# Split weights at staggered addresses in a two-layer encoder: 64 bytes for the MLPs' upward products, 192 for the value projection

## The chip, the cores and the metric

The kernel runs on one core of one Trainium2 chip. The metric is the time of one execution on the device in microseconds, as the median of several runs. TensorE multiplies, VectorE, ScalarE and GpSimd do the rest, and the DMA queues of SyncE and GpSimd bring the weights.

## What is computed

An encoder of two layers over 512 tokens of width 1024, in float32. The first layer mixes by stick-breaking attention (16 heads of 64), the second by a gated linear recurrence. Behind each mixer stands an MLP of width 4096 with a squared ReLU. Cut to what matters:

```python
def reference(x, ...):
    for layer in range(2):
        h = rms_norm(x, norm_mix[layer])
        if layer % 2 == 0:
            y = stick_breaking_attention(h, sb_w_qkv[0], sb_w_o[0])   # qkv = h @ w_qkv, ..., o @ w_o
        else:
            y = rglru_block(h, rg_w_in[0], ..., rg_w_o[0])
        x = x + y
        h = rms_norm(x, norm_mlp[layer])
        x = x + squared_relu_mlp(h, mlp_w1[layer], mlp_w2[layer])
    return rms_norm(x, norm_final)

def squared_relu_mlp(h, w1, w2):
    u = jax.nn.relu(h @ w1)
    return (u * u) @ w2
```

## The kernel before

**Split products.** A float32 product is made of three in the type float32r. Each operand `a` is split into a high part `ah` (ScalarE's cast, line 213 or, in the MLPs, line 1026 by way of the recording helper at line 755) and a low part `al` (VectorE's subtraction). TensorE then adds `wh*ah`, `wl*ah` and `wh*al` into one PSUM bank. Each of the three loads its stationary operand, 128 columns, and streams its moving operand, 512 or 256 columns.

**Widths and roles.** The dense products of the attention, the recurrence and the output projections (lines 220 to 222) load weights and stream 512 tokens. The MLPs' downward products (line 1061) load activations and stream 512 columns of weights. Two kinds stream 256 columns:

- The MLPs' upward products (`up`, line 966) load weights, `wh` or `wl`, and stream 256 tokens of `xgh`, `xgl` or a sum of blocks of them (`s41`, `low`, parts of `bh` and `bl`). The MLP multiplies 2x2 blocks by seven products in place of eight (`P1` to `P7`), hence the halves of 256. One named product is 24 matmuls.
- The value projection (`v_steps`, lines 476 to 478) loads 128 tokens of `xgh` or `xgl` and streams 256 columns of weights.

**Where the weights lie.** `wh` and `wl` are tiles of 8 x 128 float32r a partition, 4096 bytes, in the pool `wpool` with four buffers for each name. They are made by `slab_parts` (the first weights), `slab` (most of the attention and the first quarter of each MLP), `weights_high` (the recurrence, where a second pool `wmore` helps) and `operand` (the MLPs' seven products, downward and upward). In this layout every operand of the split products starts on a multiple of 512 bytes in its partition.

**The squares' sums.** For the norms, `Squares.acc` and the first layer's `sums` gather sums of squares in a tile `ssq` of 2048 bytes, which has a buffer of its own in the pool `work`. The same pool has two buffers each of `sq` and `r`.

**Order.** TensorE's order is the order in which the code issues. An MLP runs in quarters: 14 named products downward, 14 upward, and so on; `prepare` makes split weights four steps ahead. The order on VectorE and ScalarE inside the MLPs is fixed by the helper `Ordered` (line 755).

Of the kernel before, what the change touches and what calls it, by code (L numbers as in the profile page):

```python
# [11 lines left out]
F32 = mybir.dt.float32  # L12
F32R = mybir.dt.float32r
# [4 lines left out]
P = 128  # L18
S = 512
D = 1024  # L20
C = D // P
# [14 lines left out]
CUT = 2  # L36
# [25 lines left out]
def hybrid_encoder(  # L62
# [28 lines left out]
    wpool = ctx.enter_context(tc.tile_pool(name="wpool", bufs=4))  # L91
    work = ctx.enter_context(tc.tile_pool(name="work", bufs=2))
# [5 lines left out]
    def bank(tag=None):  # L98
        if tag is None:
            tag = TAGS[turn[0] % len(TAGS)]  # L100
            turn[0] += 1
        return psum.tile([P, S], F32, tag=tag, name=f"ps_{tag}")

    def f(ap):
        return ap.bitcast(F32)
# [36 lines left out]
    class Squares:  # L142


        def __init__(self):
            self.acc = work.tile([P, S], F32, tag="ssq", name="ssq", bufs=1)
            self.begun = False

        def chunk(self, c, xc, last=None, pool=None, e=V):
            if not self.begun:  # L150
                self.begun = True
                A.activation(self.acc, xc, AF.Square)
            else:
                sq = (pool or work).tile([P, S], F32, tag="sq", name="sq")
                A.activation(sq, xc, AF.Square)
                with tc.issue_after(last.ins) if last else nullcontext():
                    self.last = e.tensor_tensor(self.acc, self.acc, sq, ALU.add)
# [18 lines left out]
            return rr  # L176


    def slab_parts(src, cuts):

        raw = wpool.tile([P, C, P], F32, tag="raw", name="raw", bufs=3)
        wh = wpool.tile([P, C, P], F32R, tag="wh", name="wh")
        wl = wpool.tile([P, C, P], F32R, tag="wl", name="wl")

        def fetch(i, queue=nc.sync):
            k = slice(*cuts[i : i + 2])
            queue.dma_start(out=raw[:, k, :], in_=src[:, k, :])

        def part(i, high=A.copy):
            k = slice(*cuts[i : i + 2])  # L190
            if high:
                high(wh[:, k, :], raw[:, k, :])
            if high == V.tensor_copy:
                return
            V.tensor_tensor(wl[:, k, :], raw[:, k, :], f(wh[:, k, :]), ALU.subtract)

        return wh, wl, fetch, part
# [2 lines left out]
    slabs, loads = count(), count()  # L200
    behind = [None]

    def slab(src, cut=1, ks=range(C)):
        raws = rawpools[next(loads) % len(rawpools)]
        raw = raws.tile([P, C, P], F32, tag="raw", name="raw", bufs=3 if raws is wpool else 1)
        k = slice(ks.start, ks.stop)
        nc.sync.dma_start(out=raw[:, k, :], in_=src[:, k, :])
        pool = wpools[next(slabs) % len(wpools)]
        wh = pool.tile([P, C, P], F32R, tag="wh", name="wh")
        wl = pool.tile([P, C, P], F32R, tag="wl", name="wl")  # L210
        for i in range(cut):
            k = slice(ks.start + i * len(ks) // cut, ks.start + (i + 1) * len(ks) // cut)
            A.copy(wh[:, k, :], raw[:, k, :])  # L213
            with tc.issue_after(behind[0]) if behind[0] else nullcontext():
                V.tensor_tensor(wl[:, k, :], raw[:, k, :], f(wh[:, k, :]), ALU.subtract)  # L215
        return wh, wl
# [7 lines left out]
    def dense(src, ah, al, tag=None, halves=None, ks=range(C), ps=None):  # L224

        wh, wl = halves or slab(src, ks=ks)
        ps = bank(tag) if ps is None else ps
        for k in ks:
            three(ps, ah[:, k, :], al[:, k, :], wh[:, k, :], wl[:, k, :], k == ks[0], k == ks[-1])
        return ps  # L230
# [49 lines left out]
    NB = S // P  # L280
    PAIRS = H // 2
    half = [slice(0, HD), slice(HD, P)]
    so, early = {}, {}
# [7 lines left out]
    with ExitStack() as actx:  # L291
        hp = actx.enter_context(tc.tile_pool(name="hp", bufs=2))
# [11 lines left out]
        for i in range(2):  # L304
            both = []
            for nm in ("h", "l"):
                t = sp.tile([P, 2 * P], F32R, tag=f"last{nm}{i}", name=f"last{nm}{i}")
# [10 lines left out]
        q, kh, kl, v, w = {}, {}, {}, {}, {}  # L318
# [65 lines left out]

        xcs = [home_tile(tag, n, "x0") for tag, n in HOMES]
        parts = [slab_parts(w_qk[i, 0], (0, 2, 4, 6, 8)) for i in range(2)]
        parts += [slab_parts(w, (0, 4, 8)) for w in (w_qk[0, 1], w_qk[1, 1], w_v[0, 0], w_v[0, 1])]
        first = [bank("acc") for _ in range(2)]

        sums = work.tile([P, S], F32, tag="ssq", name="ssq", bufs=1)  # L390
        odd = hp.tile([P, S], F32, tag="ks", name="odd", bufs=1)
        sqs = [sums, odd, *(sc[:, :S] for sc in scans)]
        sqs += [work.tile([P, S], F32, tag=tag, name="sq") for tag in ("sq", "sq", "r")]
# [65 lines left out]
        def v_steps(m, tags=("acc",) * NB):  # L459

            if m:
                ws = [slab(w_v[m, i], CUT) for i in range(2)]
            else:
                ws = [u[:2] for u in parts[4:]]
                for u, name in zip(parts[4:], ("root", "copy")):

                    with tc.issue_after(norm[name].ins):
                        for i in range(2):
                            u[3](i)
            ws = [[t.rearrange("p (k two) f -> p k (two f)", two=2) for t in u] for u in ws]  # L470
            for t in range(NB):
                ts = slice(t * P, (t + 1) * P)
                ps = bank(tags[t])[:, : 2 * P]
                for k in range(C):
                    wh, wl = (u[:, k % 4, :] for u in ws[k // 4])
                    PE.matmul(ps, xgh[:, k, ts], wh, start=k == 0, stop=False)
                    PE.matmul(ps, xgh[:, k, ts], wl, start=False, stop=False)
                    PE.matmul(ps, xgl[:, k, ts], wh, start=False, stop=k == C - 1)
                    if k == C - 1:
                        vt = hp.tile([P, 4, P], F32R, tag=f"v{t}", name=f"v{t}")  # L480
                        pv = ps.rearrange("p (h d) -> p h d", h=4)
                        rc = norm["rc"][:, t : t + 1]
                        A.activation(vt[:, :, :HD], pv, AF.Identity, scale=rc)
                        V.scalar_tensor_tensor(
                            vt[:, :, HD:], pv, rc, f(vt[:, :, :HD]), ALU.mult, ALU.subtract
                        )
                        v[m, t] = vt
                    if k % 2:
                        yield
# [199 lines left out]
        steps = chain(*(g for g, _ in fill))  # L689
# [75 lines left out]
    class Mlp:  # L765
# [252 lines left out]
                self.FROM_UP,  # L1018
            )

        def operand(self, raw):
            pool = wpools[next(slabs) % len(wpools)]
            wh = pool.tile([P, C, P], F32R, tag="wh", name="wh")
            wl = pool.tile([P, C, P], F32R, tag="wl", name="wl")
            wh, wl = (t.rearrange("p (j k) f -> p j (k f)", j=2) for t in (wh, wl))
            self.A.copy(wh, raw)
            self.V.tensor_tensor(wl, raw, f(wh), ALU.subtract)
            return wh, wl
# [69 lines left out]
        def run(self, first, between, end):  # L1098
# [5 lines left out]
            steps = []  # L1104
# [5 lines left out]
            units, ws, sums, us = {("down", 0): first}, {}, {}, {}  # L1110
# [5 lines left out]
            def unit(i):  # L1116
                kind, q4, g, _ = steps[i]
                return units[kind, q4][g]

            done, made = set(), {}  # L1120
# [15 lines left out]
            def make(i):  # L1136
                if i >= len(steps):
                    return
                name = steps[i][3]
                ws[i] = made[i] = self.operand(self.source(unit(i), name))  # L1140

                for before, x in (("P5", "P7"), ("P6", "P4")):
                    if name == before:
                        self.added(unit(i), x)
# [107 lines left out]

            waiting, later = [], []
            make(0)
            add(1)
            make(1)
# [122 lines left out]
    with ExitStack() as rctx:  # L1379
# [36 lines left out]
        r = None  # L1416
# [3 lines left out]
        ws = {"c2": third}  # L1420
        raws, fetched, made = {}, count(), count(3)
# [6 lines left out]

        def weights_high(key):
            pool = wmore if next(made) % 6 > 3 else wpool  # L1430
            wh = pool.tile([P, C, P], F32R, tag="wh", name="wh")
            wl = pool.tile([P, C, P], F32R, tag="wl", name="wl")
            ws[key] = wh, wl
            OA.copy(wh, raws[key])

# [58 lines left out]
        def high(c):  # L1494

            i = C - 4 + c % 4
            gin[c] = bh[:, i, :], bl[:, i, :]
            OA.copy(gin[c][0], xc[c])
# [78 lines left out]
        for k in range(C):  # L1577
            for c in range(4):
                ps, wh, wl = begun[c]
# [6 lines left out]
    with ExitStack() as mctx:  # L1586
        lp = mctx.enter_context(tc.tile_pool(name="last", bufs=1))
# [26 lines left out]

        A.activation(lp.tile([P, 1], F32, tag="rt", name="early"), eps_t, AF.Sqrt)

        ss = lp.tile([P, 104], F32, tag="ss", name="ss")[:, : 3 * NB]
        ss = ss.rearrange("p (t i) -> p t i", t=NB)
        bias = lp.tile([P, NB], F32, tag="bias", name="bias")

# [155 lines left out]
```

## Time and profile before

| | |
|---|---|
| median of 3 runs | 1042.69 us (1041.5 to 1043.37) |
| profiled execution | 1044.21 us, span 1042.4 us |
| granted TensorE clock, mean | 0.999 |
| upward products, line 966 | 2016 matmuls, 243.4 us |
| downward products, line 1061 | 1356 matmuls, 307.5 us |
| value products, lines 476 to 478 | 3 x 128 matmuls |
| VectorE, ScalarE busy | 82%, 67% |

The upward stages lie from 331 to 371, 409 to 450 and 488 to 528 us in the first MLP, and from 799 to 841, 879 to 919 and 957 to 998 us in the second. Between and beside them lie the downward stages, before 292 us the attention, and from 567 to 759 us the recurrence. A matmul's length in the profile is modelled, from its start to the end of its last column, and the next one starts before it ends; the pace is read from the distance of starts.

### The profile page before, as it was taken

How to read it: one execution, taken by the hardware profiler on the slowest of the kernel's cores; microseconds unless marked ns; L12 is line 12 of the kernel's file. 1: busy time of each engine (PE TensorE's matmuls, PEld its weight loads, DVE VectorE, ACT ScalarE, POOL GpSimd, SP SyncE). 2: the span in 40 equal slices, each digit the busy share in tenths (PEclk: the TensorE clock that was granted, in tenths of full speed). 3: DMA queues.
4: the chain of work that ended last, by engine and by line, in shares of the span. 5: the costliest groups of instructions: out<-in, count | busy, mean ns of one | idle time of the engine just before them, and what ended most of it. 6: DMA issues, size and time to landing. Idle time of an engine off the chain costs nothing.

```text
span 1042.4 us, 15858 instructions
## 1 busy us (share of the span) xinstructions
PE 1032.3 (99%) x5862; PEld 906.2 (87%) x5862; DVE 859.0 (82%) x1148; ACT 701.6 (67%) x1083; POOL 172.5 (17%) x239
## 2 busy tenths in 40 slices
PE   9999999999999999999999999999999999999997
PEld 7888888888888988988988888888888988988986
DVE  7888787848788898898899888984789798898897
ACT  6777676836776773773765799964755773863866
POOL 0444444410010010010011121200000010010013
PEclk9999999999999999999999999999999999999999
DMA  7744454528546667667682575353446677677553
GB/s 242 209 117 142 111 152 104 160 93 294 139 78 188 184 136 205 162 137 200 152 222 78 153 189 144 102 222 90 93 80 173 173 143 199 163 144 196 150 128 109
DMA packets 53260, 160.46 MB, mean 154 GB/s; under 512 B 6720, under 2 KB 8256, under 8 KB 53184
## 3 DMA queue, kind: packets, MB, share of 16 engines
q1 hardware_dynamic: 42096, 120.35, 35.5%
q0 software_dynamic: 10656, 38.80, 22.8%
q8 instruction: 46, 0.75, 0.3%
q10 hardware_dynamic: 432, 0.31, 0.1%
q14 instruction: 30, 0.25, 0.1%
HBM read 137.41 MB, written 4.19 MB: 136 GB/s over the span
## 4 chain that ended last, share of the span: by engine, by line
PE 89%; DVE 4%; DMA 2%; ACT 2%; issue 2%; POOL 0%; SPq 0%; ACTq 0%; DVEq 0%; POOLq 0%
PE ps_t L1061 14%; PE ps_acc L966 8%; PE ps_z L966 8%; PE ps_acc L1061 7%; PE ps_o L966 5%; PE ps_acc L220 5%; PE ps_acc L222 5%; PE ps_acc L221 5%; PE ps_z L1061 4%; PE ps_t L220 2%; PE ps_t L222 2%; PE ps_t L221 2%; PE ps_o L220 2%; PE ps_o L222 2%; PE ps_o L221 2%
## 5 line engine op out<-in xcount | busy, mean ns | idle before, releaser
L755 ACT CAST wh<-b 128x1024 fp32r<-128x1024 f32 x168 | 174.3, 1049 | 126.2 <-DVE b L755 56.8
L755 DVE TENSOR_TENSOR wl<-b,wh 128x1024 fp32r<-128x1024 f32 x168 | 203.5, 1220 | 48.7 <-ACT wh L755 48.2
L1043 POOL DMA_DIRECT2D b<-in_w_dn x40 | 35.0, 874 | 364.1 <-DVE b L755 204.4
L220 PE MATMUL ps_acc<-xgh,wh 128*128 128x512 f32 x192 | 78.5, 409 | 0.0
L222 PE MATMUL ps_acc<-xgl,wh 128*128 128x512 f32 x192 | 75.2, 392 | 0.0
L221 PE MATMUL ps_acc<-xgh,wl 128*128 128x512 f32 x192 | 75.1, 391 | 0.0
L215 DVE TENSOR_TENSOR wl<-raw,wh 128x512 fp32r<-128x512 f32 (+2 forms) x70 | 61.5, 906 | 15.0 <-ACT wh L213 14.8
L579 DVE TENSOR_TENSOR_SCAN scan<-keep,later 128x128 f32<-128x128 f32 (+1 forms) x64 | 59.9, 939 | 16.8 <-ACT keep L569 12.2
L755 ACT ACTIVATE u<-u 128x512 f32<-128x512 f32 x100 | 63.1, 632 | 4.3 <-DVE u L755 2.7
L213 ACT CAST wh<-raw 128x512 fp32r<-128x512 f32 (+2 forms) x70 | 50.6, 758 | 20.2 <-PE ps_acc L222 7.3
L583 POOL TENSOR_TENSOR w<-w,scan 128x128 f32<-128x128 f32 (+1 forms) x64 | 51.8, 811 | 55.7 <-DVE scan L579 50.8
L1043 POOL DMA_DIRECT2D b<-in_w_up x24 | 20.8, 868 | 241.3 <-DVE b L755 73.1
L755 DVE TENSOR_TENSOR b<-b,b 128x1024 f32<-128x1024 f32 x48 | 58.7, 1223 | 1.3
L755 DVE TENSOR_TENSOR u<-u 128x512 f32<-128x512 f32 (+1 forms) x92 | 54.9, 596 | 2.7 <-ACT u L755 1.1
L966 PE MATMUL ps_z<-xgh,wh 128*128 128x256 f32 x192 | 54.3, 283 | 0.0
L966 PE MATMUL ps_z<-xgh,wl 128*128 128x256 f32 x192 | 54.3, 283 | 0.0
L966 PE MATMUL ps_acc<-low,wh 128*128 128x256 f32 x192 | 54.3, 283 | 0.0
L755 ACT CAST wh<-raw 128x1024 fp32r<-128x1024 f32 x46 | 48.1, 1047 | 8.4 <-PE ps_acc L1061 8.3
L1061 PE MATMUL ps_t<-wl,sh 128*128 128x512 f32 x126 | 49.2, 391 | 0.0
L1061 PE MATMUL ps_t<-wh,bh 128*128 128x512 f32 x126 | 49.2, 390 | 0.0
L1061 PE MATMUL ps_t<-wl,bh 128*128 128x512 f32 x126 | 49.1, 390 | 0.0
L1061 PE MATMUL ps_t<-wh,sh 128*128 128x512 f32 x126 | 49.0, 389 | 0.0
(399 smaller groups left out, 3428.3 us busy)
## 6 DMA issues: line engine op xcount, KB each, us to landing
b<-in_w_dn SPq DMA_DIRECT2D x48, 512.0 KB, 4.4
b<-in_w_dn POOLq DMA_DIRECT2D x40, 512.0 KB, 5.7
b<-in_w_up SPq DMA_DIRECT2D x36, 512.0 KB, 4.7
b<-in_w_up POOLq DMA_DIRECT2D x24, 512.0 KB, 5.5
raw<-in_w_m SPq DMA_DIRECT2D x16, 512.0 KB, 4.3
raw<-in_w_dn SPq DMA_DIRECT2D x16, 512.0 KB, 4.7
raw<-in_w_in SPq DMA_DIRECT2D x16, 512.0 KB, 4.3
raw<-in_w_qk SPq DMA_DIRECT2D x12, 512.0 KB, 3.7
```

The source lines that it names most:

```text
L213: A.copy(wh[:, k, :], raw[:, k, :])
L215: V.tensor_tensor(wl[:, k, :], raw[:, k, :], f(wh[:, k, :]), ALU.subtract)
L220: PE.matmul(ps, wh, ah, start=start, stop=False)
L221: PE.matmul(ps, wl, ah, start=False, stop=False)
L222: PE.matmul(ps, wh, al, start=False, stop=stop)
L579: V.tensor_tensor_scan(sc[:, S - n : S][:, ::-1], keep[:, :n][:, ::-1], later[:, S - n :][:, ::-1], 1.0, ALU.mult, ALU.max,)
L583: G.tensor_tensor(wt, wt, sc[:, S - n + 1 : S + 1], ALU.mult)
L755: ins = getattr(self.e, name)(*args, **kwargs)
L966: PE.matmul(ps[:, i * HS : (i + 1) * HS], m, y, start=new and i == k == n == 0, stop=i == 1 and k == C // 2 - 1 and n == 2, skip_group_che ...
L1043: G.dma_start(out=unit[b].rearrange("p j n -> p (j n)"), in_=unit["src"](to), accum_op=ALU.add)
L1061: PE.matmul(ps, m, y[:, jj, cols], start=first and n == 0, stop=last and n == 2, skip_group_check=not new,)
```

## The change

1. The tiles `wh` and `wl` of `wpool` are 64 elements (256 bytes) longer, 4352 bytes, and the weights are written `at` elements behind the tile's start: 16 elements (64 bytes) for the upward products, 48 elements (192 bytes) for the value projection, 0 for all others. Tiles of other pools are as before.
2. The sums of squares have no buffer of their own in `work`: `Squares.acc` takes one of the two buffers `r`, and `sums` of the first layer one of the pool `hp`'s `early`. The 2048 bytes are what the eight longer tiles need.
3. In the last stage the tile `ss` is 40 elements in place of 104, so that the second MLP's pools begin 256 bytes earlier, at a multiple of 256 that is none of 512.

The order of instructions on each engine is the same. Cut to its core:

```diff
         def __init__(self):
-            self.acc = work.tile([P, S], F32, tag="ssq", name="ssq", bufs=1)
             self.begun = False
         def chunk(self, c, xc, last=None, pool=None, e=V):
             if not self.begun:
                 self.begun = True
+                self.acc = work.tile([P, S], F32, tag="r", name="ssq")
                 A.activation(self.acc, xc, AF.Square)
...
+    ROOM, UP_AT, V_AT = 64, 16, 48
+
+    def half_slab(pool, tag, at=0):
+
+        if pool is not wpool:
+            return pool.tile([P, C, P], F32R, tag=tag, name=tag)
+        t = pool.tile([P, C * P + ROOM], F32R, tag=tag, name=tag)
+        return t[:, at : at + C * P].rearrange("p (c f) -> p c f", c=C)
+
-    def slab_parts(src, cuts):
+    def slab_parts(src, cuts, at=0):
...
-        wh = wpool.tile([P, C, P], F32R, tag="wh", name="wh")
-        wl = wpool.tile([P, C, P], F32R, tag="wl", name="wl")
+        wh = half_slab(wpool, "wh", at)
+        wl = half_slab(wpool, "wl", at)
...
-        parts += [slab_parts(w, (0, 4, 8)) for w in (w_qk[0, 1], w_qk[1, 1], w_v[0, 0], w_v[0, 1])]
+        parts += [slab_parts(w_qk[i, 1], (0, 4, 8)) for i in range(2)]
+        parts += [slab_parts(w_v[0, i], (0, 4, 8), V_AT) for i in range(2)]
...
-        sums = work.tile([P, S], F32, tag="ssq", name="ssq", bufs=1)
+        sums = hp.tile([P, S], F32, tag="early", name="ssq")
...
-                ws = [slab(w_v[m, i], CUT) for i in range(2)]
+                ws = [slab(w_v[m, i], CUT, at=V_AT) for i in range(2)]
...
-                ws[i] = made[i] = self.operand(self.source(unit(i), name))
+                at = UP_AT if steps[i][0] == "up" else 0
+                ws[i] = made[i] = self.operand(self.source(unit(i), name), at)
...
-        ss = lp.tile([P, 104], F32, tag="ss", name="ss")[:, : 3 * NB]
+        ss = lp.tile([P, 40], F32, tag="ss", name="ss")[:, : 3 * NB]
```

`slab`, `operand` and `weights_high` make their tiles by `half_slab` in the same way.

More of the change, by code (lines that the diff above doesn't have):

```diff
@@ L201, in hybrid_encoder, with slab @@
     behind = [None]
-    def slab(src, cut=1, ks=range(C)):
+    def slab(src, cut=1, ks=range(C), at=0):
         raws = rawpools[next(loads) % len(rawpools)]
@@ L208, in slab @@
         pool = wpools[next(slabs) % len(wpools)]
-        wh = pool.tile([P, C, P], F32R, tag="wh", name="wh")
-        wl = pool.tile([P, C, P], F32R, tag="wl", name="wl")
+        wh = half_slab(pool, "wh", at)
+        wl = half_slab(pool, "wl", at)
         for i in range(cut):
@@ L1019, in from_down, with operand @@
             )
-        def operand(self, raw):
+        def operand(self, raw, at):
             pool = wpools[next(slabs) % len(wpools)]
-            wh = pool.tile([P, C, P], F32R, tag="wh", name="wh")
-            wl = pool.tile([P, C, P], F32R, tag="wl", name="wl")
+            wh = half_slab(pool, "wh", at)
+            wl = half_slab(pool, "wl", at)
             wh, wl = (t.rearrange("p (j k) f -> p j (k f)", j=2) for t in (wh, wl))
@@ L1430, in weights_high @@
             pool = wmore if next(made) % 6 > 3 else wpool
-            wh = pool.tile([P, C, P], F32R, tag="wh", name="wh")
-            wl = pool.tile([P, C, P], F32R, tag="wl", name="wl")
+            wh = half_slab(pool, "wh")
+            wl = half_slab(pool, "wl")
             ws[key] = wh, wl
```

## The prediction

> **What bounds the kernel now.** I read the page's first part, then busy time by stretches, then the chain that ended last, then single products in order of time. First the page and the granted clock:
>
> ```profile
> span 1042.4 us, 15858 instructions
> PE 1032.3 (99%) x5862; PEld 906.2 (87%) x5862; DVE 859.0 (82%) x1148; ACT 701.6 (67%) x1083; POOL 172.5 (17%) x239
> PEclk9999999999999999999999999999999999999999
> ```
>
> TensorE is busy 99% of the span at a full clock, so a change is worth what it takes from or adds to TensorE's own pace, unless another engine then falls behind. The profiled execution took 1044.21 us beside a span of 1042.4; the median of the runs shown is 1042.69, 1.5 below it. I work with differences and apply them to the median.
>
> The next view gives busy time in an upward stage, a downward stage, and the first upward stage of the second MLP (columns: stretch, length, then busy time and count for PE, PEld, DVE, ACT and POOL, clock, DMA share, GB/s). The rows under it are all PE and PEld work of line 966, the upward products, over the whole span.
>
> ```profile
> 409.00:449.50 40.50, 40.50 (x339) 40.46 (x338) 31.94 (x32) 29.39 (x39) 3.54 (x5) 1.00 0.61 152
> 449.50:487.50 38.00, 38.00 (x170) 31.48 (x169) 35.77 (x41) 19.82 (x25) 4.30 (x5) 1.00 0.78 186
> 798.60:840.70 42.10, 40.83 (x337) 40.41 (x336) 35.53 (x38) 30.02 (x41) 3.46 (x4) 1.00 0.60 149
> ...
> 0.00:1042.40 1042.40, 243.37 (x2016) 242.82 (x2016) 1.00 0.59 154
> ```
>
> In an upward stage TensorE and its weight loads have no gap at all, while VectorE is idle for 8.6 us of 40.5. VectorE is closest to its limit downward, 35.8 of 38.0. There are 2016 upward products, 23% of the span. The chain that ended last (start, length, what) shows their pace beside that of the downward ones:
>
> ```profile
> 409.34 14.39 PE ps_acc L966 x120
> 423.73 2.88 PE ps_z L966 x24
> 463.28 5.44 PE ps_t L1061 x24
> 804.10 7.27 DMA b<-in_w_up
> ```
>
> Twenty-four products of 256 columns take 2.88 us, so one starts every 120.0 ns; twenty-four of 512 columns take 5.44 us, 226.7 ns each. The difference, 106.7 ns for 256 columns, is 0.417 ns a column. What is left, 120.0 - 106.7 and 226.7 - 213.4, is **13.3 ns beside the columns in each product, at either width**. Every product loads new weights of 128 columns while the one before streams. A weight load that costs the stream a fixed number of ns would look just like that. Since the cost doesn't grow with the columns, it weighs 11% in a 256-wide product and 6% in a 512-wide one.
>
> **What moves, and whether the 13.3 ns can move.** The order of instructions on every engine is the same before and after, and so are the waits, but for one: GpSimd's first addition into the squares at the end of the first MLP no longer waits for TensorE. What changes is addresses. Before, every operand of these products starts on a multiple of 512 bytes. After, the loaded weights of line 966 start 64 bytes past a multiple of 256, and the streamed weights of lines 476 to 478 start 192 bytes past one. In the value products the roles are exchanged, so the loaded operand stands 64 bytes past the streamed one, modulo 256, in both. No trace of before shows a product at such an address, so I bound the effect by how far the fixed part moves without a change of shape. In order of time (start, length, engine, line), three places in the attention:
>
> ```profile
> 36.22 0.28 PE L476 MATMUL ps_acc<-wh,xgh 128*128 128x256 f32 x1
> ...
> 38.97 0.28 PE L560 MATMUL ps_z<-kh,q 128*128 128x256 f32 x1
> ...
> 87.24 0.28 PE L476 MATMUL ps_acc<-wh,xgh 128*128 128x256 f32 x1
> 87.35 0.27 PE L477 MATMUL ps_acc<-wl,xgh 128*128 128x256 f32 x1
> 87.47 0.28 PE L478 MATMUL ps_acc<-wh,xgl 128*128 128x256 f32 x1
> 87.58 0.28 PE L476 MATMUL ps_acc<-wh,xgh 128*128 128x256 f32 x1
> ...
> 212.84 0.40 PE L220 MATMUL ps_acc<-bh,wh 128*128 128x512 f32 x1
> ...
> 215.15 0.39 PE L221 MATMUL ps_z<-bh,wl 128*128 128x512 f32 x1
> ```
>
> The first pair is 23 steps apart: 2.75 us, 119.6 ns each, the usual pace. But right behind 512-wide products three steps of 256 columns take 0.34 us, 113 ns each, and in the last pair ten steps of 512 columns take 2.31 us, 231 ns against 226.7. So the fixed part is no constant of the instruction: same shapes, same 512-byte grid, and it goes from about 7 to about 18 ns with how the streams happen to lie in time to each other. I assume that the load and the stream hinder each other by where they stand to each other, and that a shift in address then acts as a shift in time does. In the upward stages they have settled into 13.3 ns, which for 256 columns is on the bad side of what these rows show.
>
> The Trainium skill, "TensorE: Matmul & The Clock Gate", Part 2, speaks against this: the stream and the weight load have independent read ports into the SBUF, and loading the next weights doesn't take read bandwidth from the running product. By that rule the change is worth nothing. Its "Back-to-back issue gap" section gives N/2.4 + 2.5 ns, which would be 109.2 and 215.8 where the rows have 120.0 and 226.7; the trace disagrees by 10.8 ns a product.
>
> **The sum.** Bounds of the step of a 256-wide product after the change: below, 110 ns, two starts 0.11 us apart in the second place above; above, 126.7, as much over 120.0 as 113.3 is under it. I take 113.3, the mean of the three steps at 87 us, since it is the short pace that this very shape shows.
>
> - Upward products: 2016 x 6.7 ns = 13.4 us less. At the bounds: 20.2 less, 13.5 more.
> - Value products: these are the rows of lines 476 to 478, counted here for one of the three:
>
> ```profile
> 0.00:1042.40 1042.40, 36.87 (x128) 24.31 (x128) 1.00 0.59 154
> ```
>
>   3 x 128 = 384 products, from 119.6 to 113.3 at best: 2.4 us. They are mixed with score and attention products that keep their addresses, and some run short already; I count half, 1.2 us.
> - What is late next: an upward and a downward stage together take 78.5 us, in which VectorE works 31.9 + 35.8 = 67.7. At the new pace they take 76.3, and VectorE still has 8.6 us to spare. ScalarE has more (29.4 + 19.8 busy). So in five of the six upward stages the whole gain should stand. In the sixth, 798.6 to 840.7, TensorE does wait:
>
> ```profile
> PE ps_z L966 <- ACT u L755: 1.0, 1, 1.0
> PE ps_acc L966 <- ACT u L755: 0.2, 1, 0.2
> ```
>
>   There a late transfer (the 7.27 us of DMA in the chain above) sets the pace, and a faster TensorE waits longer. Of that stage's 336 x 6.7 = 2.2 us I give back 1.1.
> - Tiles of 4352 bytes in the pool instead of 4096, casts and subtractions at shifted addresses: nothing. They stay contiguous, and the 8.6 us of idle VectorE in an upward stage cover some 0.5 us for each of its 14 or so subtractions.
> - The squares' buffers: nothing. The tiles come from rings whose earlier readers are long done, and no engine but GpSimd has a wait changed. The wait it loses was not the one that held it:
>
> ```profile
> POOL ssq L157 <- ACT sq L155: 22.8, 2, 22.0
> ```
>
> Together 13.4 + 1.2 - 1.1 = 13.5 us less: 1042.7 - 13.5 = **1029.2 us**. With the skill's 2.5 ns in place of 13.3 for the 2400 products the sum would be some 26 us less, 1017, an estimate from its page.
>
> **Rivals.**
>
> *The reads don't meet at all* (so the 13.3 ns is a fixed price of changing weights, and addresses are idle): 1042.7, within 0.2% (2.1 us, about what a measurement of this kernel can tell from no change). For it: the sameness of 120.0 in every upward stage, and the skill's two ports named above. Against it: 113 and 231 at the same shapes and addresses. It is also the case in which the change doesn't do what it says. 12%.
>
> *The stagger falls on the wrong side*: the settled step of the 256-wide products goes up instead of down. Price: 126.7 instead of 120.0 in 2016 products, 13.5 us more, and 1.2 in the value products: 1057.4. It decides from any step above 120, at 2.4 us for each ns. For it: the last pair above shows that the fixed part does go up to 18 ns. Against it: that was at 512 columns; the 256-wide rows shown that leave the settled pace are shorter. 12%.
>
> *The 512-byte grid is lost*: a tile of 4352 bytes puts every second buffer of split weights at 256 past a multiple of 512, and the second MLP's pool moves by 256 too. By the layout that touches 1461 of the 2868 512-wide products of the dense and downward lines. If the settled 226.7 needs the grid and becomes the 231 of the attention, that is 1461 x 4.3 ns = 6.3 us more: 1049.0 if the stagger brings nothing, 1035.5 if it brings the 13.5. For it: all of before lies on that grid. Against it: nothing in the trace shows a difference between 512 and 256, and the unsettled rows lie on the grid as well. 8% for the slower of the two.
>
> **How the numbers follow.** The forecast's direction, with steps anywhere from 110 to 118 ns and with or without a loss on the grid, has 68%; its likeliest point is 1029.2. No change 12%, slower 12 + 8 = 20%. The low end is the 110 ns step in all: 20.2 + 3.7 (384 x 9.6), so 1042.7 - 23.9, about 1018. Upward the range goes over no change to the lost grid, 1050; only the wrong side of the stagger lies beyond it. Faster by over 0.2% 0.68, within 0.12, slower 0.20.
>
> **What would show it.** In the profile after: twenty-four upward products in 2.72 us instead of 2.88, an upward stage of 38.1 us instead of 40.3, downward ones still at 5.44 for twenty-four. A mean length of the same PE rows is modelled and says less than the distance of starts. If 2.88 stays, the ports don't meet; 3.04 is the wrong side; 5.5 or more for twenty-four downward products is the grid. If the step is 113 and the time falls by much less than 13 us, a new wait of line 966 on VectorE or ScalarE must show.

## The result and the profile after

| | before | after |
|---|---|---|
| median of 6 runs | 1042.83 us (1041.5 to 1044.0) | 1039.26 us (1038.68 to 1040.07) |
| profiled execution, span | 1044.21, 1042.4 us | 1039.09, 1037.4 us |

The ratio is 0.9967 (0.9954 to 0.998): the change makes the kernel about 3.5 us faster, a quarter of the 13.5 forecast. The two profiled executions differ by 5.1 us, since the one of before lies above its median; stage by stage I compare these two.

The chain of waits of after (start, length, what), two upward runs and the second half of the downward stage on either side:

```profile
382.31 5.73 PE ps_t L1071 x24
388.03 5.44 PE ps_acc L1071 x24
...
407.07 14.13 PE ps_acc L976 x120
421.21 2.83 PE ps_z L976 x24
...
460.27 5.73 PE ps_t L1071 x24
```

The upward products are now line 976, the downward ones 1071, the recording helper 765. The 120 products at 409.34 in before took 14.39 us and take 14.13; 24 took 2.88 and take 2.83. That is 117.8 ns a step instead of 120.0, and it is that in every product of five stages: each falls from 40.31 to 39.57 us. The sixth, first of the second MLP, falls from 42.10 to 40.51; it starts at 117.8 too, but TensorE waits twice in it, and behind the second wait some 125 of its steps take 113 or 114 ns. All upward stages together: 5.3 us less.

A downward row got longer. 5.44 us stood at 463.28 in before; at its place after, 460.27, stand 5.73. TensorE's weight loads (PEld) wait there. The waits of before, then those of after (us in total, times, longest):

```profile
PEld ps_z L1061 <- DVE wl L755: 0.9, 2, 0.5
PEld ps_t L1061 <- DVE wl L755: 0.6, 2, 0.3
```

```profile
PEld ps_t L1071 <- DVE wl L765: 2.6, 6, 0.7
PEld ps_z L1071 <- DVE wl L765: 1.2, 3, 0.4
PEld ps_acc L1071 <- DVE wl L765: 0.3, 1, 0.3
```

Four waits on VectorE's low part `wl` have become ten. One of them in order of time, at the seventh named product of the first downward stage behind an upward one; first VectorE and TensorE in before:

```profile
385.95 2.36 DVE L755 TENSOR_TENSOR wl<-b,wh 128x1024 fp32r<-128x1024 f32 x2 [0.57 <-ACT wh L755]
...
387.41 0.39 PE L1061 MATMUL ps_t<-wh,sh 128*128 128x512 f32 x1
387.64 0.39 PE L1061 MATMUL ps_t<-wl,sh 128*128 128x512 f32 x1
```

The same instructions in after:

```profile
383.96 2.36 DVE L765 TENSOR_TENSOR wl<-b,wh 128x1024 fp32r<-128x1024 f32 x2 [0.57 <-ACT wh L765]
...
384.86 0.39 PE L1071 MATMUL ps_t<-wh,sh 128*128 128x512 f32 x1
385.25 0.50 PE L1071 MATMUL ps_t<-wl,sh 128*128 128x512 f32 x1
```

The row of VectorE is two subtractions of 1.18 us, and the product `wl,sh` needs the first. In before it was done at 387.13, half a microsecond ahead of its use. TensorE reaches this place 2.55 us earlier than before (384.86 against 387.41), VectorE only 1.99 (383.96 against 385.95). The slack is gone, and the step before `wl,sh` is 0.39 us instead of 0.23. Over the whole kernel, from the first start of each part to that of the next: upward 5.3 less, attention 1.8 less (1.2 of it in the value products), recurrence unchanged, downward stages 2.0 **more**. That sums to the 5.1 between the profiled runs.

### The profile page after: what moved, and what is told of

Read it like the earlier page. It is cut to its first block, busy times and chain, and to the rows that moved or that the text cites. A ratio compares the mean times of both kernels' runs of the same rounds, so it can differ in the third digit from the quotient of the medians.

```text
span 1037.4 us, 15857 instructions
## 1 busy us (share of the span) xinstructions
PE 1027.6 (99%) x5862; PEld 899.8 (87%) x5862; DVE 858.8 (83%) x1148; ACT 702.0 (68%) x1083; POOL 172.4 (17%) x239
## 4 chain that ended last, share of the span: by engine, by line
PE 90%; DVE 5%; ACT 2%; issue 2%; DMA 1%; ACTq 0%; DVEq 0%; POOL 0%; POOLq 0%
PE ps_t L1071 14%; PE ps_acc L976 8%; PE ps_z L976 7%; PE ps_acc L1071 7%; PE ps_acc L229 5%; PE ps_acc L231 5%; PE ps_acc L230 5%; PE ps_o L976 4%; PE ps_z L1071 3%; PE ps_t L229 2%; PE ps_t L231 2%; PE ps_t L230 2%; DVE wl L765 2%; PE ps_o L229 2%; PE ps_o L231 2%; PE ps_o L230 2%
## 5 line engine op out<-in xcount | busy, mean ns | idle before, releaser
L1071 PE MATMUL ps_t<-wh,sl 128*128 128x512 f32 x126 | 49.1, 389 | 0.0
```

The lines of the kernel that those rows point to most:

```text
L1071: PE.matmul(ps, m, y[:, jj, cols], start=first and n == 0, stop=last and n == 2, skip_group_check=not new,)
```

## The experiments

Two theories stood. **Pace**: the step depends on where the loaded operand starts against the streamed one, 113.3 ns is to be had, but the kernel settles in another state. **Late next**: whatever TensorE gains upward, VectorE takes back part of it downward. The first rival was that addresses are idle and the 3.5 us come from elsewhere in the change.

**1. The pace by itself.** A kernel of TensorE's products alone:

```diff
+    for name in AT:                      # weights 0, 16, 32 ... 256 bytes behind a 512-byte start
+        for d in (0, 4, 8, 12):
+            phase(d)                     # one product of 384 + d columns, another entry
+            products(name, 256, 30)      # 30 products of the kernel's form, 256 columns
```

and the same at 512 columns, with the streamed operand shifted in the weights' place, and with both shifted.

> A kernel of matmuls alone (it computes none of the reference's output): triples of products as in the change, 256 or 512 columns streamed, the loaded weights 0, 16, 32, 48, 64, 96, 128, 160, 192, 224 and 256 bytes past a multiple of 512, each run of 30 products entered at four moments 4 columns apart. If the address of the loaded operand against the streamed one sets the pace (theory), runs at 0 and 256 bytes settle at the same 120.0 ns a step, runs at 64 at about 117.8 or 113.3 ns depending on the moment of entry, and some other distance does better than 64. If the step is a fixed price and the 117.8 of the change came from the moment alone (rival), the same set of paces shows at every distance. A stream shifted by 192 bytes should act as a load shifted by 64. For 512 columns the theory expects 226.7 at 0 and more elsewhere, since the change leaves those at 0.

The chain of waits, runs of 30 products behind four entries each: weights at distance 0, then 64 bytes, then 192 bytes (one of four).

```profile
25.89 3.60 PE ps L55 x30
...
29.67 3.58 PE ps L55 x30
...
33.43 3.59 PE ps L55 x30
...
37.20 3.60 PE ps L55 x30
...
85.83 3.42 PE ps L55 x30
...
89.44 3.40 PE ps L55 x30
...
93.02 3.54 PE ps L55 x30
...
96.73 3.40 PE ps L55 x30
...
145.26 3.53 PE ps L55 x30
```

3.60 us for 30 is 120 ns each, 3.54 is 118, 3.40 is 113. Each entry ran once. The distances of starts over the last 18 of each run:

| loaded start minus streamed start, bytes | 0 | 16 | 32 | 48 | 64 | 96 | 128 | 160 | 192 | 224 | 256 |
|---|---|---|---|---|---|---|---|---|---|---|---|
| step, 256 columns, ns | 120.0 | 118.5 | 118.2 | 118 (once 123.3) | 113.3, once 117.8 | 117.2 to 118.9 | 118.6 to 118.9 | 120.0 | 117.8 | 116.4 to 117.8 | 120.0 |

At 512 columns the step settles at 226.7 ns at distance 0 and 256, takes 228.8 at 192, and 232 to 234 at every other distance. With the streamed operand shifted by 192 instead, the step is that of 64 (113.3 in three of four entries, 117.8 in one); shifted by 64, that of 192 (117.8); with both shifted by 64, 120.0. So the pace depends on the distance of the two starts modulo 256 bytes. The fit is not perfect: with 64 bytes under the load and 192 under the stream, which is distance 128 again, one entry gave 118.4 and the other 120.0. The expected distance with a step shorter than at 64 bytes did not show up. The rival that addresses are idle is out, and so is a fixed price of a weight load. And 64 bytes have **two** settled paces; three of the four entries lead to 113.3, and the kernel runs at the other.

**2. Which entry leads where.** Finer distances, each entered from 15 settled products of 512 columns, as an upward stage is: straight, or behind one extra product of 256, 260, 264 or 268 columns.

```diff
-            phase(d)
-            products(name, 256, 30)
+            products("zero", 512, 15)
+            if d:                        # 0, 256, 260, 264, 268
+                nudge(name, d)
+            products(name, 256, 24)
```

> Matmuls alone again (none of the reference's output): each distance of 52, 56, 60, 64, 68, 72, 80, 224 and 240 bytes is entered as the kernel enters an upward stage, from settled 512-wide products at distance 0, either straight or behind one extra product of 256, 260, 264 or 268 columns. Theory, that the distance decides which paces exist and the moment of entry which of them holds: 64 bytes shows 117.8 ns straight and 113.3 behind at least one of the extra products, and the other distances their own pace near 118 to 120. Rival, that 113.3 belongs to the entry from a 384-wide product only: 117.8 in all five entries at 64.

At 64 bytes the straight entry gives 117.8, 256, 264 and 268 give 117.8, and 260 gives 113.3. At 52 bytes three of the five entries give 113.3, but the straight one gives 120.0. All other distances tried (56, 60, 68, 72, 80, 224, 240 bytes) stay between 116.4 and 120.0. Of these, 224 bytes takes 116.4 to 116.9 ns from all five entries, the straight one among them, which is shorter than the 117.8 of 64 bytes behind the straight entry; in experiment 1 one of four entries gave 117.8 there. The chain at 64 bytes; each row is the 24 narrow products behind an extra one of 256, 260 or 264 columns and the 15 wide ones that follow:

```profile
131.33 6.25 PE ps L55 x39
...
137.71 6.15 PE ps L55 x39
...
143.98 6.26 PE ps L55 x39
```

The middle one is 0.10 us shorter, 24 steps of about 4.5 ns. The straight entry is the kernel's case: each upward stage comes out of settled 512-column products, so each begins at 117.8.

**3. The value projection alone**, with the longer tiles kept:

```diff
-    ROOM, UP_AT, V_AT = 64, 16, 48
+    ROOM, UP_AT, V_AT = 64, 0, 48
```

> The change with the upward products' weights back at 0 bytes; longer tiles, pools and the value projection's 192 bytes stay. If the upward stagger carries the gain (theory), 2016 products return to 120.0 ns a step, the 0.3 us wait at each downward stage goes, and the gain shrinks from 3.5 to about 1.2 to 1.8 us: 1041.2. If the tiles' new places lose the 512-byte grid's pace (rival), downward products take more than 5.44 us for 24 and the time is at or over 1042.8.

1041.91 against 1042.93 us, ratio 0.9989 (0.998 to 0.9998): 1.0 us, about the forecast's 1.2. Its chain:

```profile
323.48 5.44 PE ps_t L1071 x24
328.92 14.39 PE ps_acc L976 x120
```

With the upward shift undone, 14.39 is back. The wide downward products stand at 5.44 though half the weight buffers no longer start on a multiple of 512 bytes: the lost grid costs nothing.

**4. The state set inside the kernel.** One extra product, whose result is overwritten, ahead of each upward stage, with widths 256, 260, 264, 268, 268, 262:

```diff
+        NUDGE = (256, 260, 264), (268, 268, 262)
...
-        def up(self, name, w, ps, new):
+        def up(self, name, w, ps, new, nudge=0):
+            if name == "P1" and nudge:
+                PE.matmul(ps[:, :nudge], w[0][:, 0, :P], xgh[:, 0, :nudge], start=True, stop=True)
...
-                self.up(name, ws.pop(i), banks[to], new)
+                self.up(name, ws.pop(i), banks[to], new, self.NUDGE[self.layer][q4 - 1] * (g == 0))
```

> The change, with one extra product (its sum is overwritten by the next) ahead of the first of each upward stage: 256, 260, 264 columns in the first MLP's three, 268, 268, 262 in the second's. Theory: at least one of these stages settles at 113.3 ns, 38.1 us in place of 39.57, and VectorE, which then has about 1.5 us less for the same work, makes TensorE wait longer in the downward stage behind it than the 0.3 us now. Rival (the moment doesn't matter in the kernel): all stages stay at 39.57 plus about 0.12 for the extra product.

Widths 260 and 262 turn the whole stage to 113.3 ns: 38.45 and 38.47 us without the extra product, where 256, 264 and, in the fifth stage in order of time, 268 leave 39.58. The downward stage behind 260 takes 39.11 us where the same one in after takes 38.39, and the last one, behind 262, 38.84 against 38.19 from first to last start: of the 1.1 us gained upward, 0.7 go back at once. The total says nothing (one run, 1044.42 us): at the first stage of the second MLP the extra product itself read a tile that was cast late,

```profile
PEld ps_acc L973 <- ACT xgh L765: 4.5, 1, 4.5
```

and for 6 us after that wait TensorE's granted clock was 0.50 (last section). Behind this, the rest of that stage ran at 113.3 ns too, though its extra product has 268 columns.

**5. The short state in all six stages**: width 260 everywhere, from another part of `xgh`.

```diff
-        NUDGE = (256, 260, 264), (268, 268, 262)
+        NUDGE = (260, 260, 260), (260, 260, 260)
...
-                PE.matmul(ps[:, :nudge], w[0][:, 0, :P], xgh[:, 0, :nudge], start=True, stop=True)
+                PE.matmul(ps[:, :nudge], w[0][:, 0, :P], xgh[:, 4, :nudge], start=True, stop=True)
```

> The change with one extra product of 260 columns, whose sum the next product overwrites, ahead of each of the six upward stages; it streams columns that nothing rewrites. Theory, that the moment of entry chooses between two settled paces: all six stages take about 38.45 us in place of 39.57 (-6.7 in all), and the downward stage behind each has its second and third wait on VectorE back, about 0.7 us each, so some 0.4 net a stage: 2 to 2.5 us under the change, 1037. Rival, that faster upward products are worth their full size: 6.5 us under the change, 1032.8.

1038.31 against 1043.10 us, ratio 0.9953 (0.9941 to 0.9965). This is the lowest time of a kernel that leaves nothing out, about 1 us below after, with overlapping intervals. Its chain and its waits:

```profile
407.45 10.90 PE ps_acc L981 x96
...
432.03 3.09 PE ps_z L981 x24
```

```profile
PEld ps_t L1076 <- DVE wl L765: 3.3, 6, 0.7
PEld ps_z L981 <- ACT u L765: 2.4, 6, 0.8
```

Ninety-six products in 10.90 us are 113.5 ns each. Then, ahead of the tenth named product, TensorE waits for ScalarE's `u` (at 432 us 0.26 us more than a step). The row of 3.09 us begins behind the wait; it holds one step of 226 ns, then steps of 117.8, and runs to the end of its last product. All six stages have such a wait. Behind it two stay at 113 (38.62 and 38.46 us with the wait) and three fall to 117.8 (38.98 each); the first stage of the second MLP had fallen in its second named product already (40.89). So the state can change at a wait, and a faster TensorE makes the wait. It need not change: in experiment 11 all six stages have this wait, and all six run at 113.3 behind it.

**6 to 8. VectorE relieved by a transfer.** One of VectorE's additions in each of the eight downward stages done by an adding transfer of GpSimd's queue (`FARS` is its list), with the extra products, without them, and in before:

```diff
-            FARS = [("P6", 0)]
+            FARS = [("P6", 0), ("P5", 1)]
```

> As the one with the extra products, and in each downward stage one of VectorE's additions of raw weights (1.22 us, P5 of the second half) becomes a DMA that adds while it lands. If VectorE early in the downward stage gives the gain back (theory), its waits there fall to about nothing, downward stages return to 38.1 us, and the time falls to about 1033. If the extra 512 KB read in each of eight stages costs more than that (rival), a wait on a DMA appears and the time stays at or over 1037.

> The change with only that addition moved to a DMA. Theory: the 0.3 us wait in each downward stage behind an upward one goes (six stages, one of them 0.8), about 2 us under the change: 1037.3. Rival (the waits are not VectorE's): same as the change, 1039.3.

> The kernel before with only that addition moved to a DMA, to see what the move is worth by itself. There downward stages behind upward ones hardly wait, so theory expects no more than 0.5 us under before: 1042.4; a DMA that comes late would show as slower.

All three failed: 1057.28 (ratio 1.0135, 1.0121 to 1.0149), 1057.23 (1.014, 1.0122 to 1.0158) and 1059.84 us (1.0161, 1.0144 to 1.0178). In before with that transfer, waits that before did not have:

```profile
PEld ps_acc L1061 <- ACT wh L755: 8.6, 6, 4.4
PEld ps_acc L1061 <- DVE wl L755: 7.4, 8, 1.1
```

ScalarE's casts wait for such transfers eight times, 31.0 us in all, where in before it is 1.4 us in two places:

```profile
ACT wh L755 <- DMA b<-in_w_dn: 31.0, 8, 7.8
```

The transfer arrives later than VectorE's addition did, and what is split from it is late too. These runs tell nothing about VectorE's share.

**9 to 11. VectorE relieved by leaving work out.** The additions ahead of `P5` in the downward stages are not done; before, after, and the kernel of experiment 5:

```diff
                     done.add(i)
+                    if what[0] == "down" and name == "P5":
+                        return
                     self.added(unit(i), name, far=far)
```

> The kernel before, leaving out VectorE's additions of raw weights for P5 downward (two of 1.22 us in each of eight stages, so these products use the wrong weights). It is the base for the next two. Both theories: downward stages behind upward ones didn't wait on VectorE, so the time stays within 1 us of before, 1042 to 1043.

> The change with the same additions left out. Theory, that VectorE early in the downward stage takes back part of what the upward stages gain: the waits of 0.3 us behind each upward stage go, downward stages return to 38.11 us, and the difference to the kernel before with the same left out is about 6 x 0.74 + 1 = 5.4 us in place of 3.5. Rival (the waits have another cause, ScalarE's casts or the DMAs): they stay, and so does the 3.5.

> The change with the extra products and the same additions left out. Theory: upward stages at 38.2 to 38.5 us, downward at 38.1 without waits: 6 x 1.9 + 1 = about 12 us under the kernel before with the same left out, so 1030 to 1031, the size that the forecast had. Rival (TensorE meets another wait as soon as it is faster): no more than 6 us.

| | us | ratio to before |
|---|---|---|
| before, less the additions | 1041.77 | 0.9988 (0.9979 to 0.9998) |
| after, less the additions | 1036.25 | 0.993 (0.9913 to 0.9946) |
| extra products, less the additions | 1034.38 | 0.9914 (0.9899 to 0.9929) |

Without these additions the same change of addresses is worth 5.5 us instead of 3.5, and the stages say why. In the second row no downward stage behind an upward one is longer than in before (38.11 where after has 38.4), none of the waits on `wl` of line 1071 is left, and at the place where after had 5.73 stands

```profile
382.35 5.44 PE ps_t L1071 x24
```

Five upward stages are at 39.57 in both, and the sixth at 40.51 and 40.59. So the 2 us of longer downward stages are VectorE's. (By the whole times alone, 5.5 and 3.5 are not apart within their intervals; the stages carry this.) The third row met its expectation only in part, 7.4 us below the first instead of 12, though 1965 of its 2016 upward steps are at the short pace of 112 to 114 ns:

```profile
PEld ps_z L981 <- ACT u L765: 4.0, 6, 2.4
PEld ps_t L1076 <- DVE wl L765: 2.9, 5, 0.6
```

At 113.3 ns TensorE reaches the next limit: ScalarE's `u` upward, 2.4 us of it in the first stage of the second MLP, and still VectorE at the seventh product downward, 0.5 us in each of five stages.

**12. The addition on GpSimd.** In the kernel of experiment 5, the addition of `P5` in the second half goes to GpSimd as an instruction, five steps ahead:

```diff
-                self.V.tensor_tensor(unit[b], unit[b], unit[to], ALU.add)
+                (G if pool else self.V).tensor_tensor(unit[b], unit[b], unit[to], ALU.add)
...
+                pool = what[0] == "down" and (name, what[2]) == ("P5", 1)
```

> The change with the extra products, and in each downward stage one of those additions (P5 of the second half) done by GpSimd in place of VectorE; all results kept. If GpSimd, mostly idle, takes it without holding up the DMAs that it issues (theory), the waits on VectorE shrink by up to 1.2 us a stage and the time falls to 1034 to 1036. If the addition comes late there, at some 3 us, or the queued DMAs do (rival), a wait on GpSimd or on a DMA shows at the fifth product downward and the time is over 1038.

A miss: 1045.62 us, ratio 1.0022 (1.0012 to 1.0032). A new wait stands first in the list:

```profile
PEld ps_t L1076 <- DVE sl L765: 7.1, 6, 1.3
```

It stands at the third product of the six downward stages behind an upward one. The trace shows what is late there: VectorE's subtraction `sl` beside GpSimd's addition, one of the six places:

```profile
452.05 2.15 DVE L765 TENSOR_TENSOR sl<-u,sh 128x512 fp32r<-128x512 f32 x1 [0.88 <-ACT sh L765]
```

```profile
451.26 2.39 POOL L1062 TENSOR_TENSOR b<-b,b 128x1024 f32<-128x1024 f32 x1 [1.85 <-DVE wl L765]
```

Six of these subtractions of 128x512 run while GpSimd adds, and they take 2.15 us; the 36 others take 0.69. In the kernel of experiment 5 `sl` starts 4.5 us behind the start of this stage and takes 0.69, here 4.7 us and 2.15. So it is hardly the order: the subtraction itself lasts three times as long beside GpSimd's addition. Why is not shown.

## Why the prediction was right and wrong

**Right: the fixed part moves with addresses.** Experiment 1 turns on nothing else and gets 113.3 to 123.3 ns from one instruction. This also decides the page's rule that stood against the change: the Trainium skill, "TensorE: Matmul & The Clock Gate", Part 2, gives stream and weight load independent ports. The measured steps depend on how the two start against each other, so by these runs the two are not independent. (The formula of its "Back-to-back issue gap" section stands there for an isolated product, so the 10.8 ns that the prediction set against it is no test of it.) Right too were the value products (1.2 forecast; 1.0 by experiment 3), the buffers (nothing), and that the grid would not decide.

**Wrong: "I take 113.3."** The term of 13.4 us is 2016 x 2.2 = 4.4 at the settled 117.8, and 5.3 with the short steps and the shorter waits in the sixth stage. (4.4, and 1.2 from the value products, less 2.0 downward are 3.6, the difference of the medians; the rest of the 5.1 between the profiled runs is 0.9 in the sixth stage and 0.6 in the attention, and the latter varies: in the other profiled runs with the upward weights at 64 bytes the attention is 1.3 to 2.7 shorter than in before.) The number 113.3 came from three steps behind wide products in the attention, before anything had settled, and at distance 0. It was the right value of one state at 64 bytes by chance, and not of the state that the kernel falls into. The bound of 118 stood in the forecast's own case ("anywhere from 110 to 118") and in the range; the point did not use it. The first step that failed is the assumption "that a shift in address then acts as a shift in time does". In experiment 1 a shift in time at distance 0 does not last: all four entries come back to 120.0 within the 30 products. A shift in address stays, and has settled paces of its own, 113.3 and 117.8. Three unsettled steps can't tell which of them a long stage reaches.

**Wrong: "VectorE still has 8.6 us to spare ... the whole gain should stand."** This is the second step that failed. That was VectorE's work summed over an upward and a downward stage. Short stretches of before show it otherwise (stretch, length, busy time and count of PE, PEld, DVE, ACT, POOL, clock, DMA share, GB/s):

```profile
409.34:419.00 9.66, 9.66 (x82) 9.66 (x82) 5.99 (x6) 5.32 (x8) 0.87 (x1) 1.00 0.58 131
...
439.00:449.60 10.60, 10.60 (x90) 10.60 (x90) 10.00 (x11) 8.62 (x14) 1.05 (x2) 1.00 0.55 159
449.60:457.00 7.40, 7.40 (x35) 6.09 (x34) 7.09 (x9) 6.74 (x11) 1.58 (x2) 1.00 0.90 155
457.00:464.00 7.00, 7.00 (x32) 5.82 (x31) 6.80 (x9) 1.95 (x3) 0.86 (x1) 1.00 0.62 143
```

VectorE's idle time lies at the start of the upward stage (3.7 of 9.7 us), where it waits for ScalarE's cast `wh`. From the stage's last quarter into the downward stage it works 23.9 of 25.0 us. In after the same place reads

```profile
437.00:446.60 9.60, 9.60 (x83) 9.60 (x83) 9.54 (x10) 7.71 (x12) 0.89 (x1) 1.00 0.60 173
446.60:454.00 7.40, 7.40 (x35) 6.09 (x34) 6.54 (x8) 6.90 (x11) 1.74 (x2) 1.00 0.92 152
454.00:461.00 7.00, 7.00 (x32) 5.81 (x31) 7.00 (x10) 1.67 (x4) 0.86 (x1) 1.00 0.63 139
```

with hardly any idle left at the end of the upward stage, none in the stretch of the wait, and 0.9 us between, 0.6 of it for ScalarE's cast `sh`. VectorE's work is not the whole of it: the late `wl` shown above follows 0.57 us in which VectorE waits for ScalarE's cast of a sum that VectorE has just added. What experiment 10 shows is that the additions in this chain cost the 2 us. What is late next was the right question, and the new wait was looked for on the wrong scale: 0.3 us in four of the six downward stages behind an upward one, 0.8 in one, next to nothing in the last, 2.0 in all. At 113.3 the forecast would have failed for this reason too: experiment 5 has that pace in two thirds of the upward steps (1331 of 2016) and wins 4.8 us, and the last kernel of experiments 9 to 11, with nearly all of them there and VectorE relieved, wins 7.4 against before with the same left out.

**The sixth stage.** Half of its gain was to be lost; it gained 1.6 us, more than any other: 0.7 by the settled pace, some 0.6 by the short steps behind its second wait, and 0.3 since the two waits got shorter. (The one of 1.0 us shrank to 0.6, the one of 0.2 grew to 0.4; the rest lies in the steps behind them.)

**The rivals.** "The reads don't meet" and "the wrong side" are out by experiment 1, the lost grid by experiment 3. None of them was the way in which the number missed. (The range's low end, 1042.7 - 23.9, is 1019 and not 1018; nothing rests on it.) What happened would have been a fourth case: the right direction, a smaller settled step, and a busy neighbour that takes 2 us of it.

**Open.** Why the period is 256 bytes and why one distance has two settled paces is not shown by any run. A distance of 224 bytes, whose 116.7 ns from the straight entry would take some 2016 x 1.1 = 2.2 us more off the upward stages by an estimate from experiment 2, was not tried in the kernel, and VectorE may take part of that back. A distance of 52 bytes, which reached 113.3 from three of five entries but not from the straight one, was not tried there either.

## What to carry to other kernels

Where products load new weights each time, measure the step for a few distances between the starts of the loaded and the streamed operand, by themselves, at the kernel's width, in runs long enough to settle and from the entry that the kernel has; a step seen a few times in passing is no forecast. Before counting a gain of the bounding engine as whole, look at the second busiest engine in stretches of a few microseconds at the place where the gain arrives, not at its average over the stage. Here the shorter pace alone brought about 1 us more (experiment 5), and VectorE's two additions a stage, left out, about 3 us (experiment 10), so the next gain lies first in VectorE's work around the change from upward to downward.

## What was not expected of the hardware

- The pace of a product with a new weight load depends on the distance of the two operands' starts modulo 256 bytes, and the best distance depends on the width: at 512 columns 0 is the best of those tried (226.7 ns) and 64 bytes takes 233; at 256 columns 0 gives 120.0 and 64 bytes 113.3 or 117.8.
- At a distance of 64 bytes the settled pace has two values, and which one holds is decided by what ran just before: an extra product of 260 columns ahead of a stage takes 4.5 ns off each product of the stage behind it (38.45 instead of 39.58 us a stage), one of 256 or 264 does not. Behind a wait of some 0.3 us the short pace was lost in three stages of experiment 5 and kept in two, and kept in all six of experiment 11.
- VectorE's subtraction of 128x512 takes 0.69 us, and 2.15 us beside an addition of 128x1024 on GpSimd (experiment 12).
- After TensorE had stood 4.0 us in experiment 4, its granted clock was 0.50 in the stretch behind the wait:

```profile
800.00:803.00 3.00, 3.00 (x16) 3.00 (x15) 2.54 (x4) 0.61 (x1) 0.87 (x1) 0.50 0.41 30
```
